# The last three experts of a mixture in plain fp32, from weights that are no longer split

## The chip, the cores and the metric

The kernel runs on one core of a Trainium2 chip. The metric is the device time of one execution in microseconds. Before the change it is 2594.24 us (median of 3 runs, 2590.64 to 2599.49). The five engines are named as in the profile: PE (TensorE), ACT (ScalarE), DVE (VectorE), POOL (GpSimd) and SP (SyncE), which here issues nearly all DMAs.

## What is computed

Four transformer blocks in a row, for one sequence of 256 tokens and a width of 1024, all in fp32. The change reaches the last part of the last block alone, a mixture of eight experts in which every token is sent to two:

```
def swiglu(h, w_gate, w_up, w_down):
    return (jax.nn.silu(h @ w_gate) * (h @ w_up)) @ w_down

def moe_swiglu(h, router, w_gate, w_up, w_down):          # h: 1 x 256 x 1024
    t = h.reshape(-1, d)
    logits = (t @ router).astype(jnp.float32)
    top_v, top_i = lax.top_k(logits, TOP_K)                # TOP_K = 2, N_EXPERTS = 8
    top_w = jax.nn.softmax(top_v, axis=-1)
    gates = jnp.sum(jax.nn.one_hot(top_i, N_EXPERTS, dtype=jnp.float32) * top_w[..., None], axis=1)
    out = jnp.zeros(t.shape, jnp.float32)
    for e in range(N_EXPERTS):
        y_e = swiglu(t, w_gate[e], w_up[e], w_down[e]).astype(jnp.float32)
        out = out + gates[:, e:e + 1] * y_e
    return out.astype(h.dtype).reshape(bsz, seq, d)
```

An expert has three matrices of 1024 x 3584 (gate, up) and 3584 x 1024 (down) in fp32, 44 MB together; all eight are 352 MB.

## The kernel before

**Places.** The experts are put in the order of how many tokens they have. The tokens of an expert are gathered by a product with a one-hot matrix (`moe_gather`, line 2171) into so many places: 128 for each of the first five experts, 64 for each of the last three (`PLACES`, line 1980). Below, the first are the wide experts, the last the narrow ones. A second pass for tokens that found no place is in the program, but does not run with this input.

**Weights.** An expert's matrices come in 42 loads of 1 MiB each, SBUF tiles of 128 partitions by 2048 fp32 values (line 217, issued by SP in program order). For gate and up a load holds two blocks of 128 rows by 1024 columns, in an expert's last step four blocks by 512. After landing in a `raw` buffer, ACT rounds the tile to fp32r (`wh`, line 222), and DVE takes what is left over (`wl = raw - wh`, line 223). After that `raw` is free, and SP may issue the next load into it. There are five `raw` buffers, three `wh` and three `wl` (`phase` with two more opened by `wider`, lines 2383, 2388 and 2401).

**Products.** An operand is a sum of two fp32r parts, too. For a wide expert three products are made, high by high, high by rest, rest by high (`mm3`, lines 229 to 231), 128 columns of the stationary operand by 512 moving ones. For a narrow expert the 64 columns of both parts of the tokens stand side by side in one stationary operand of 128 columns, and two products with `wh` and with `wl` (line 2263) leave two halves of the PSUM partitions, 0 to 63 and 64 to 127, which are folded by a copy and an add (`whole`, lines 2286 and 2287, tile `eb`). A load thus costs 12 products with a wide expert and 8 with a narrow one.

**Order.** An expert's 3584 hidden columns are done in four steps (three of 1024, one of 512). Step i goes: gate product of step i + 1, transposes of step i's hidden values (`turn`, line 2311), up product of step i + 1, down product of step i. At the end of an expert `combine` brings its rows back to the tokens with four pairs of products (lines 2347 and 2348) and adds them, weighted, to the sum (line 2349). So the first narrow expert's first 8 loads stand ahead of the last 2 loads of the last wide expert. The kernel ends with the four stores of line 2167.

**Other places that are referred to.** Lines 727, 728, 751 and 752 belong to an earlier block and are not touched. They are plain fp32 products: line 727 is one product of 128 stationary by 256 moving columns, line 728 one by 128; lines 751 and 752 are, for each of two heads, a product of 64 stationary columns by 256 (751) and by 128 (752) moving ones, the first head's result in PSUM partitions 0 to 63, the second's in 64 to 127.

Of the kernel before, what the change touches and what calls it, by code (L numbers as in the profile page):

```python
# [22 lines left out]
ND = 8  # L23
# [31 lines left out]
class Core:  # L55
# [65 lines left out]
    @contextmanager  # L121
    def phase(s, raw, split, work):

        with ExitStack() as c:
            pool = lambda nm, n: c.enter_context(s.tc.tile_pool(name=f"{nm}{s.uid()}", bufs=n, reuse_waits="tile"))
            s.ring = {nm: [pool(nm, n)] * n for nm, n in (("raw", raw), ("wh", split), ("wl", split))}
            s.t2p = pool("t2", work)
            yield

    @contextmanager  # L130
    def wider(s, **more):

        with ExitStack() as c:
            for nm, n in more.items():
                p = c.enter_context(s.tc.tile_pool(name=f"{nm}{s.uid()}", bufs=n, reuse_waits="tile"))
                s.ring[nm].extend([p] * n)
            s.turn = 0
            yield

    turn = 0  # L140
# [1835 lines left out]
class MoE:  # L1976
# [125 lines left out]
    def moe(s, N):  # L2102
# [6 lines left out]
        s.moe_pass(N, N.slot, s.PLACES, s.TOGETHER, first, ahead)  # L2109
# [3 lines left out]
        with s.tc.If(n > 0):  # L2113
            rest = s.small([128, 2, s.E], "slotb")
            nc.vector.tensor_sub(rest, N.slot, bc(s.caps, 2))
            s.moe_pass(N, rest, s.REST, s.TOGETHER_REST, s.moe_gather(N, rest, s.TOGETHER_REST[0], s.REST))
            s.moe_store()
# [52 lines left out]
    def moe_gather(s, N, slot, js, places):  # L2170
# [20 lines left out]
        for d in range(0, ND, 2):  # L2191
            p = s.psum("b")
            for m in range(2):
                for h, src in enumerate((N.H, N.L)):
                    for t in range(2):
                        nc.tensor.matmul(p[:, m * W:m * W + W], src[d // 2][:, t, m * 128:m * 128 + 128], P[:, t, :W],
                                         start=(h == 0 and t == 0 and m == 0), stop=(h == 1 and t == 1),
                                         skip_group_check=True)
            for m in range(2):
                x = s.t2([128, 512], "xe", F32R)  # L2200
                x = x[:, :2 * W].rearrange("p (a j c) -> p j a c" if wide else "p (j a c) -> p j a c", a=2, j=len(js))
                v, g = p[:, m * W:m * W + W].rearrange("p (j c) -> p j c", j=len(js)), s.col("ln_ffn_2", 8 + d + m)
                nc.scalar.activation(x[:, :, 0], v, AF.Copy, scale=g)
                nc.vector.scalar_tensor_tensor(x[:, :, 1], v, g, f(x[:, :, 0]), op0=OP.mult, op1=OP.subtract)
                X.append(x)
        return {j: [X, i, places[j], P] for i, j in enumerate(js)}

    def moe_places(s, N, G):
# [4 lines left out]
        n = next(iter(G.values()))[2]  # L2213
        for X, i, n, P in G.values():
            for t in range(2):
                nc.tensor.matmul(p[:n, i:i + 1], f(P[:, t, i * n:i * n + n]), N.rc[:, t:t + 1], start=(i == 0 and t == 0),
                                 stop=(t == 1), skip_group_check=True)
        nc.vector.tensor_copy(rc[:n], p[:n, :len(G)])
        for g in G.values():
            X, i, n, P = g  # L2220
            PT = s.t2([128, 2, 128], "onehotT", F32R)
            x = P[:, :, i * n:i * n + n]
            if n == 64:
                y = s.t2([128, 512], "eyH", F32R)[:, :256].rearrange("p (t c) -> p t c", t=2)
                for u in range(2):
                    nc.vector.tensor_copy(y[:, :, u * 64:u * 64 + 64], f(x))
                x = y
            p = s.psum("b", dt=F32R)
            for t in range(2):
                nc.tensor.transpose(p[:, t * 128:t * 128 + 128], x[:, t], s.identR)  # L2230
            nc.scalar.copy(PT, p[:, :256].rearrange("p (t c) -> p t c", t=2))
            g += [PT, rc[:n, i:i + 1]]

    AHEAD = 3
    WIDE = 1024

# [4 lines left out]
    def moe_pass(s, N, slot, places, together, G, ahead=()):  # L2241
# [3 lines left out]
        steps = [(j, f0, min(s.WIDE, s.FE - f0)) for j in range(s.E) for f0 in range(0, s.FE, s.WIDE)]  # L2245
        per = len(steps) // s.E
        py = {}
        ahead = list(ahead)
        most = places is s.PLACES
        src = {nm: I[f"o_moe_w_{nm}_2"][0] for nm in ("gate", "up", "down")}  # L2250

        def weights(nm, j, *a):
            e = N.expert[j]
            w = src[nm]
            return s.weights(w[e] if isinstance(e, int) else w[bass.ds(e, 1)].rearrange("o r c -> (o r) c"), *a)

        def product(o, j, x, w, start, stop):


            if x.shape[2] == 64:  # L2260
                x = x.rearrange("p a c -> p (a c)")
                for h in range(2):
                    nc.tensor.matmul(o, x, w[h], start=start and h == 0, stop=stop and h == 1, skip_group_check=True)  # L2263
            else:
                s.mm3(o, (x[:, 0], x[:, 1]), w, start, stop)

        def half(i, nm):

            j, f0, fn = steps[i]
            X, u = G[j][:2]  # L2270
            p = [s.psum("a") for _ in range(fn // 512)]
            nk = 2048 // fn
            for k0 in range(0, ND, nk):
                w = ahead.pop(0) if ahead else weights(nm, j, 128 * k0, nk, f0, fn)
                for k in range(nk):
                    for c, o in enumerate(p):
                        product(o, j, X[k0 + k][:, u], [x[:, k, c * 512:c * 512 + 512] for x in w],
                                k0 + k == 0, k0 + k == ND - 1)
            return p

        def whole(p, n):

            if n == 128:
                return p
# [3 lines left out]
            return a  # L2288

        def gate(i, pg):  # L2290
            n, rc = G[steps[i][0]][2], G[steps[i][0]][5]
            out = []
            for p in pg:
                out.append(s.t2([n, 512], "eh"))
                nc.scalar.activation(out[-1], whole(p, n), AF.Silu, scale=rc)
            return out

        def hidden(i, h, pu):
            n, rc = G[steps[i][0]][2], G[steps[i][0]][5]
            for x, p in zip(h, pu):  # L2300
                nc.vector.scalar_tensor_tensor(x, whole(p, n), rc, x, op0=OP.mult, op1=OP.mult)
            return h

        def turn(i, h):

            n = G[steps[i][0]][2]
            out = []
            for x in h:
                p = s.psum("b")
                for k in range(4):  # L2310
                    nc.tensor.transpose(p[:, k * n:k * n + n], x[:, k // 2 * 256 + k % 2:k // 2 * 256 + 256:2],
                                        s.ident[:n, :n])
                v = p[:, :4 * n].rearrange("p (k c) -> p k c", k=4)
                if n == 128:
                    H, L = s.t2([128, 4, n], "ehH", F32R), s.t2([128, 4, n], "ehL", F32R)
                else:
                    x = s.t2([128, 4, 2, n], "ehHL", F32R)
                    H, L = x[:, :, 0], x[:, :, 1]
                s.split(v, H, L)
                out.append((H, L) if n == 128 else x)  # L2320
            return out

        def down(i, hs):
            j, f0, fn = steps[i]
            if f0 == 0:
                py[j] = [s.psum("b"), s.psum("b")]
            for k0 in range(0, fn // 128, 2):
                w = weights("down", j, f0 + 128 * k0, 2, 0, D, "p k")
                h = hs[k0 // 4]
                for k in range(2):  # L2330
                    kk = k0 % 4 + k
                    for c in range(2):
                        wc = [x[:, k, c * 512:c * 512 + 512] for x in w]
                        start, stop = f0 == 0 and k0 + k == 0, f0 + fn == s.FE and k0 + k == fn // 128 - 1
                        if isinstance(h, tuple):
                            s.mm3(py[j][c], (h[0][:, kk, :], h[1][:, kk, :]), wc, start, stop)
                        else:
                            product(py[j][c], j, h[:, kk], wc, start, stop)

        def combine(j):  # L2340
            PT = G[j][4]
            for c in range(2):
                yH, yL = s.t2([128, 512], "eyH", F32R), s.t2([128, 512], "eyL", F32R)
                s.split(py[j][c], yH, yL)
                for t in range(2):
                    p = s.psum("b")
                    nc.tensor.matmul(p, PT[:, t, :], yH, start=True, stop=False)
                    nc.tensor.matmul(p, PT[:, t, :], yL, start=False, stop=True)
# [4 lines left out]
        pg = half(0, "gate")  # L2353
# [4 lines left out]
        h = hidden(0, h, half(0, "up"))  # L2358
        for i in range(n):
            j, f0, fn = steps[i]  # L2360
            if f0 == s.WIDE and j + 1 < s.E and j + 1 not in G:
                g = s.moe_gather(N, slot, next(x for x in together if j + 1 in x), places)
                s.moe_places(N, g)
                G |= g
            pg = half(i + 1, "gate") if i + 1 < n else None
            hs = turn(i, h)
            if pg is not None:
                h = gate(i + 1, pg)
                h = hidden(i + 1, h, half(i + 1, "up"))
            down(i, hs)  # L2370
# [58 lines left out]
```

## Time and profile before

| | |
|---|---|
| median of 3 runs | 2594.24 us |
| profiled execution | 2596.73 us, its span 2595.0 us |
| granted TensorE clock over the span | 0.968 of full speed |
| PE, DVE, ACT busy | 2423.1, 2004.4, 1550.8 us |
| read from memory | 555.88 MB, 215 GB/s over the span |

The mixture takes the last 40% of the span: the page's line of GB/s jumps from 131 to 343 in slice 26 of 40. A busy share is an average over all stages, and for DMA it says that packets were underway, not how many loads stood ready behind them. An engine's idle time only costs something where somebody waits for it; what ends a wait is in the views of waits.

### The profile page before, as it was taken

Reading aid. Unit: us, or ns where it says so; the run is one execution under the profiler, and the core shown is the slowest. Engines: PE = TensorE matmul, PEld = TensorE weight load, DVE = VectorE, ACT = ScalarE, POOL = GpSimd, SP = SyncE. Lnnn points to the kernel's source line nnn. Section 1 sums busy time; section 2 is a strip of 40 time slices with the busy share of each in tenths; the row PEclk is TensorE's granted clock in tenths of the full one; section 3 lists DMA queues with packets and bytes.
Section 4 is the critical chain, followed back from the end, with each engine's and each line's share of the span. In section 5 each row is a group of like instructions: output and inputs, shape, how many; then the busy total and the mean of one; then the engine's idle time right before and its main releaser. Section 6 shows DMA issues by size and latency. Waiting matters only on the chain.

```text
span 2595.0 us, 39887 instructions
## 1 busy us (share of the span) xinstructions
PE 2423.1 (93%) x15462; PEld 2122.8 (82%) x15462; DVE 2004.4 (77%) x3186; ACT 1550.8 (60%) x2313; POOL 88.0 (3%) x180
## 2 busy tenths in 40 slices
PE   7988799999998999899999999999999999988887
PEld 6867689999888999789999888888888877655654
DVE  6876477658886765766658876888888888999998
ACT  4553355445555544564455645776777777878776
POOL 2011010000001000000000000000000000000000
PEclk9998699999999999989999998999999999999999
DMA  5312345555434555425554213999999998999997
GB/s 166 111 58 34 62 166 167 178 178 162 131 109 137 165 178 183 146 82 184 183 172 130 87 45 131 343 359 349 368 329 365 346 360 325 371 379 363 372 369 281
DMA packets 266195, 559.59 MB, mean 216 GB/s; under 512 B 12751, under 2 KB 172510, under 8 KB 251662
## 3 DMA queue, kind: packets, MB, share of 16 engines
q1 hardware_dynamic: 264544, 555.71, 61.2%
q0 software_dynamic: 1328, 1.22, 0.9%
q8 instruction: 123, 2.02, 0.3%
q14 instruction: 74, 0.61, 0.1%
q10 hardware_dynamic: 126, 0.03, 0.0%
HBM read 555.88 MB, written 1.05 MB: 215 GB/s over the span
## 4 chain that ended last, share of the span: by engine, by line
PE 69%; DVE 15%; issue 6%; ACT 4%; POOL 2%; DMA 2%; DVEq 0%; ACTq 0%; POOLq 0%; SPq 0%
PE pa L230 16%; PE pa L231 16%; PE pa L229 16%; DVE wl L223 9%; ACT wh L222 2%; PE pb L230 2%; PE pb L231 2%; PE pb L229 2%; PE pb L1167 2%; PE pb L1792 2%; PE pa L2263 1%; PE pb L1481 1%; PE pb L2263 1%; PE pb L1133 1%; DMA ssmvb<-in_ssm_a_log_dram 1%
## 5 line engine op out<-in xcount | busy, mean ns | idle before, releaser
L223 DVE TENSOR_TENSOR wl<-raw,wh 128x512 fp32r<-128x512 f32 (+1 forms) x1108 | 1258.7, 1166 | 212.3 <-ACT wh L222 207.1
L222 ACT CAST wh<-raw 128x512 fp32r<-128x512 f32 (+1 forms) x1108 | 1063.6, 1004 | 559.3 <-issue 266.3
L229 PE MATMUL pa<-xH,wh 128*128 128x256 f32 (+1 forms) x1936 | 553.2, 286 | 16.0 <-ACT xH L313 8.1
L230 PE MATMUL pa<-xL,wh 128*128 128x256 f32 (+1 forms) x1936 | 553.3, 286 | 0.5 <-DVE xL L314 0.5
L231 PE MATMUL pa<-xH,wl 128*128 128x256 f32 (+1 forms) x1936 | 552.8, 286 | 1.0 <-DVE wl L223 1.0
L229 PEld LDWEIGHTS pa<-xH,wh 128*128 128x128 f32 (+1 forms) x1936 | 372.3, 193 | 18.1 <-ACT xH L313 8.8
L230 PEld LDWEIGHTS pa<-xL,wh 128*128 128x128 f32 (+1 forms) x1936 | 372.3, 192 | 3.5 <-DVE xL L314 2.0
L231 PEld LDWEIGHTS pa<-xH,wl 128*128 128x128 f32 (+1 forms) x1936 | 372.2, 192 | 2.9 <-DVE wl L223 1.9
L230 PE MATMUL pa<-wl,xe 128*128 128x512 f32 x560 | 221.1, 395 | 7.7 <-DVE wl L223 7.7
L231 PE MATMUL pa<-wh,xe 128*128 128x512 f32 x560 | 219.7, 392 | 0.0
L229 PE MATMUL pa<-wh,xe 128*128 128x512 f32 x560 | 207.7, 393 | 0.0
L2263 PE MATMUL pa<-wl,xe 128*128 128x512 f32 x336 | 131.2, 424 | 36.8 <-DVE wl L223 34.0
L229 PE MATMUL pa<-hidH,wh 128*128 128x256 f32 x528 | 149.4, 283 | 0.0
L230 PE MATMUL pa<-hidL,wh 128*128 128x256 f32 x528 | 149.4, 283 | 0.0
L231 PE MATMUL pa<-hidH,wl 128*128 128x256 f32 x528 | 149.4, 283 | 0.0
L230 PEld LDWEIGHTS pa<-wl,xe 128*128 128x128 f32 x560 | 105.7, 189 | 34.0 <-DVE wl L223 12.8
L2263 PE MATMUL pa<-wh,xe 128*128 128x512 f32 x336 | 123.7, 402 | 3.5 <-ACT wh L222 3.5
L229 PEld LDWEIGHTS pa<-wh,xe 128*128 128x128 f32 x560 | 105.6, 189 | 21.3
L231 PEld LDWEIGHTS pa<-wh,xe 128*128 128x128 f32 x560 | 105.6, 189 | 21.0
L2263 PEld LDWEIGHTS pa<-wl,xe 128*128 128x128 f32 x336 | 59.6, 192 | 76.3 <-DVE wl L223 67.0
L230 PE MATMUL pb<-wl,ehH 128*128 128x512 f32 x280 | 111.2, 397 | 0.9 <-DVE wl L223 0.9
L231 PE MATMUL pb<-wh,ehL 128*128 128x512 f32 x280 | 109.4, 391 | 0.0
(813 smaller groups left out, 4078.8 us busy)
## 6 DMA issues: line engine op xcount, KB each, us to landing
raw<-in_o_moe_w_gate_dram SPq DMA_DIRECT2D x112, 1024.0 KB
raw<-in_o_moe_w_up_dram SPq DMA_DIRECT2D x112, 1024.0 KB
raw<-in_o_moe_w_down_dram SPq DMA_DIRECT2D x112, 1024.0 KB
raw<-in_ffn_w_dram SPq DMA_DIRECT2D x60, 1024.0 KB
raw<-in_od_w_in_dram SPq DMA_DIRECT2D x20, 1024.0 KB
raw<-in_o_w_in_dram SPq DMA_DIRECT2D x16, 1024.0 KB
raw<-in_e_ffn_w_gate_dram SPq DMA_DIRECT2D x11, 1024.0 KB
raw<-in_e_ffn_w_up_dram SPq DMA_DIRECT2D x11, 1024.0 KB
```

The lines of the kernel that those rows point to most:

```text
L222: nc.scalar.copy(H[:, c:e], raw[:, c:e])
L223: nc.vector.tensor_sub(L[:, c:e], raw[:, c:e], f(H[:, c:e]))
L229: mm(out, a[0], b[0], start=start, stop=False, skip_group_check=True)
L230: mm(out, a[0], b[1], start=False, stop=False, skip_group_check=True)
L231: mm(out, a[1], b[0], start=False, stop=stop, skip_group_check=True)
L1133: nc.tensor.matmul(p[:, k * 128:k * 128 + 128], NT[:, k, :], X[:, k, :], start=True, stop=True)
L1167: mm = lambda o, a, b, st=True, sp=True: nc.tensor.matmul(o, a, b, start=st, stop=sp, skip_group_check=True)
L1481: mm = lambda o, a, b, st, sp: nc.tensor.matmul(o, a, b, start=st, stop=sp, skip_group_check=True)
L1792: mm = lambda o, a, b, st=True, sp=True: nc.tensor.matmul(o, a, b, start=st, stop=sp, skip_group_check=True)
L2263: nc.tensor.matmul(o, x, w[h], start=start and h == 0, stop=stop and h == 1, skip_group_check=True)
```

## The change

For a narrow expert a load is no longer split. `whole_weights` loads it, and PE reads it as it lies there, in plain fp32. The gathered tokens are kept as one fp32 tile (`xf`) of 64 columns an expert. A row block of a load now gives two products of 64 stationary columns: one half of the moving columns goes to PSUM partitions 0 to 63, the other half to 64 to 127. SiLU and product then run on [128, 512] tiles at once; four transposes bring them to `ehT`. Since nothing is split, the `wh` and `wl` buffers can take loads as well: `KINDS` gives the order in which loads go to the eleven buffers, each ring with its own turn (`buffer`). `moe_gather` and `moe_places` double the one-hot matrix, so that both halves find their rows; `combine` uses plain fp32 products with 64 rows. The wide experts' code does as before; the second pass is called in another way and still does not run.

```
+    def buffer(s, nm):
+        i = s.turns[nm]
+        s.turns[nm] += 1
+        return s.ring[nm][i % len(s.ring[nm])].tile([128, 2048], F32 if nm == "raw" else F32R, tag=nm,
+                                                    name=f"{nm}{s.n}")
...
-        raw, H, L = (s.ring[nm][s.turn % len(s.ring[nm])].tile([128, 2048], dt, tag=nm, name=f"{nm}{s.n}")
-                     for nm, dt in (("raw", F32), ("wh", F32R), ("wl", F32R)))
-        s.turn += 1
+        raw, H, L = (s.buffer(nm) for nm in ("raw", "wh", "wl"))
...
+    def whole_weights(s, src, k0, nk, c0, cn, rows="k p", kind="raw"):
+        s.n += 1
+        raw = s.buffer(kind)
+        v = f(raw)[:, :nk * cn].rearrange("p (k c) -> p k c", k=nk)
+        s.nc.sync.dma_start(v, src[k0:k0 + 128 * nk, c0:c0 + cn].rearrange(f"({rows}) c -> p k c", p=128))
+        return v
...
+                else:
+                    nc.scalar.activation(y[:, m], v, AF.Copy, scale=g)
+                    X.append(y[:, m].rearrange("p (j c) -> p j c", c=64))
...
+    KINDS = ("raw", "wh", "raw", "wl", "raw", "wh", "raw", "wl", "raw", "wh", "wl")
...
+            return s.weights(w, *a) if places[j] == 128 else s.whole_weights(w, *a, kind=next(kinds))
...
-            if x.shape[2] == 64:
-                x = x.rearrange("p a c -> p (a c)")
-                for h in range(2):
-                    nc.tensor.matmul(o, x, w[h], start=start and h == 0, stop=stop and h == 1, skip_group_check=True)
...
+                        for c in range(2):
+                            mm(p[0][64 * c:64 * c + 64, :hw], X[k0 + k][:, u], w[:, k, c * hw:c * hw + hw],
+                               start=start, stop=stop, skip_group_check=True)
...
-            a = s.t2([64, 512], "eb")
-            nc.scalar.copy(a, p[64:])
-            nc.vector.tensor_add(a, p[:64], a)
...
+                    y = s.t2([128, n, 128], "ehT")
+                    nc.scalar.copy(y, v)
...
+                        for c in range(2):
+                            mm(py[j][0][64 * c:64 * c + 64], hs[0][:, q, 64 * a:64 * a + 64],
+                               w[:, k, c * 512:c * 512 + 512], start=start, stop=stop, skip_group_check=True)
...
+            if not wide:
+                y = s.t2([128, 512], "ey")
+                nc.scalar.copy(y, py[j][0])
...
+                        mm(p, f(PT[64 * c:64 * c + 64, t, :]), y[64 * c:64 * c + 64], start=True, stop=True)
```

PE's queue at the first load of the first narrow expert, before: one load, eight products, `xe` the stationary operand with both parts.

```order
L2263 MATMUL pa_22594<-wh_22597,xe_22099 128x512
L2263 MATMUL pa_22594<-wl_22598,xe_22099 128x512
L2263 MATMUL pa_22595<-wh_22597,xe_22099 128x512
L2263 MATMUL pa_22595<-wl_22598,xe_22099 128x512
L2263 MATMUL pa_22594<-wh_22597,xe_22102 128x512
L2263 MATMUL pa_22594<-wl_22598,xe_22102 128x512
L2263 MATMUL pa_22595<-wh_22597,xe_22102 128x512
L2263 MATMUL pa_22595<-wl_22598,xe_22102 128x512
```

The same place now: four products a load (x4), all to one PSUM tile, the first from a `raw` buffer, the second from a `wh` buffer, and so on; line 2335 is the transposes of the last wide step.

```order
L2307 MATMUL pa_22582<-raw_22583,xf_22099 64x512 x4
L2307 MATMUL pa_22582<-wh_22589,xf_22111 64x512 x4
L2307 MATMUL pa_22582<-raw_22595,xf_22123 64x512 x4
L2335 MATMUL pb_22607<-ident,eh_22470 128x128 x4
L2307 MATMUL pa_22582<-wl_22601,xf_22135 64x512 x4
L2307 MATMUL pa_22618<-raw_22619,xf_22099 64x512 x4
```

What stood in eight products by 512 columns, alternately with `wh` and `wl`, are now four with 64 columns from one buffer.

SP's queue at the same place, before: every load goes into a `raw` buffer, and the two last loads of the last wide expert (down) come after the narrow expert's first eight.

```order
L217 DMA raw_22596<-in_o_moe_w_gate_dram 128x2x1024
L217 DMA raw_22610<-in_o_moe_w_gate_dram 128x2x1024
L217 DMA raw_22624<-in_o_moe_w_gate_dram 128x2x1024
L217 DMA raw_22638<-in_o_moe_w_gate_dram 128x2x1024
L217 DMA raw_22673<-in_o_moe_w_up_dram 128x2x1024
```

And now (line 236 is `whole_weights`, line 222 `weights`):

```order
L236 DMA raw_22583<-in_o_moe_w_gate_dram 128x2x1024
L236 DMA wh_22589<-in_o_moe_w_gate_dram 128x2x1024
L236 DMA raw_22595<-in_o_moe_w_gate_dram 128x2x1024
L236 DMA wl_22601<-in_o_moe_w_gate_dram 128x2x1024
L236 DMA raw_22619<-in_o_moe_w_up_dram 128x2x1024
```

The loads and their order are the same; the buffers alternate, and the second load goes into a `wh` buffer.

## Rows read from the trace of the kernel before

**Rows 1.** The page: its span, and the span in 40 slices.

```profile
span 2595.0 us, 39887 instructions
...
DVE  6876477658886765766658876888888888999998
...
DMA  5312345555434555425554213999999998999997
```

**Rows 2.** Stages: stretch in us, then busy us (and instructions) by engine, clock, DMA.

```profile
core 0: us, PE busy (x) PEld busy (x) DVE busy (x) ACT busy (x) POOL busy (x), PEclk, DMA share, GB/s
2000.00:2100.00 100.00, 98.61 (x446) 81.24 (x445) 88.92 (x53) 71.67 (x49) 0.00 (x0) 1.00 0.96 353
2212.00:2570.00 358.00, 303.39 (x1161) 211.32 (x1160) 341.14 (x232) 281.47 (x219) 0.00 (x0) 0.97 0.99 373
2225.50:2583.90 358.40, 301.86 (x1146) 207.79 (x1145) 340.85 (x230) 279.66 (x218) 0.00 (x0) 0.97 0.96 362
```

**Rows 3.** Groups by line, 2225.5 to 2583.9: busy us, mean ns, idle before.

```profile
L223 DVE TENSOR_TENSOR wl<-raw,wh 128x2048 fp32r<-128x2048 f32 x127 | 285.5, 2283 | 12.1 <-ACT wh L222 11.5
L222 ACT CAST wh<-raw 128x2048 fp32r<-128x2048 f32 x126 | 237.4, 1906 | 20.3 <-PE pb L2263 8.8 <-DMA raw<-in_o_moe_w_up_dram 4.2 <-DMA raw<-in_o_moe_w_gate_dram 3.3
...
L2287 DVE TENSOR_TENSOR eb<-pa,eb 64x512 f32<-64x512 f32 x42 | 27.7, 677 | 4.1 <-ACT eb L2286 4.1
L2286 ACT COPY eb<-pa 64x512 f32<-64x512 f32 x42 | 23.4, 579 | 41.9 <-PE pa L2263 41.8
```

**Rows 4.** What SP's DMA queue waited for, 2212 to 2570: us, times, longest.

```profile
SPq L217 <- DVE wl L223: 258.3, 113, 5.1
SPq L217 <- DVE ehHL L291: 29.1, 14, 2.3
```

**Rows 5.** Short stretches of the narrow stage, and one early stretch.

```profile
2295.00:2307.00 12.00, 9.07 (x36) 6.06 (x35) 10.80 (x7) 9.62 (x8) 0.00 (x0) 1.00 1.02 421
2350.00:2370.00 20.00, 15.23 (x57) 9.73 (x56) 18.89 (x14) 17.01 (x14) 0.00 (x0) 1.00 1.02 414
2414.00:2426.00 12.00, 9.09 (x36) 6.05 (x35) 10.80 (x7) 9.62 (x8) 0.00 (x0) 1.00 1.03 424
2470.00:2484.00 14.00, 11.02 (x43) 7.29 (x42) 12.81 (x10) 11.91 (x11) 0.00 (x0) 1.00 1.02 414
2526.00:2546.00 20.00, 16.31 (x63) 10.92 (x62) 18.65 (x11) 15.79 (x14) 0.00 (x0) 1.00 1.02 416
2546.00:2556.00 10.00, 8.78 (x34) 6.54 (x33) 10.00 (x10) 8.48 (x7) 0.00 (x0) 0.83 0.98 356
2333.00:2340.00 7.00, 5.38 (x23) 3.54 (x22) 6.43 (x6) 6.97 (x6) 0.00 (x0) 1.00 0.76 243
2500.00:2514.00 14.00, 11.75 (x41) 8.24 (x40) 14.00 (x12) 11.12 (x11) 0.00 (x0) 0.88 0.92 315
274.60:322.30 47.70, 45.06 (x247) 38.20 (x248) 24.46 (x76) 17.48 (x49) 2.08 (x2) 0.61 0.20 70
```

**Rows 6.** PE in order of time, plain fp32: start us, length us, then the group.

```profile
634.50 0.60 PE L727 MATMUL pb<-bc,bc 128*128 128x256 f32 x2
634.93 0.38 PE L728 MATMUL pb<-bc,bc 128*128 128x128 f32 x2
...
647.38 0.66 PE L751 MATMUL pb<-mt,xd 128*64 128x256 f32 x4
647.86 0.40 PE L752 MATMUL pb<-mt,xd 128*64 128x128 f32 x4
```

**Rows 7.** PE in order of time: last wide loads' first product, first narrow one.

```profile
2214.89 0.39 PE L229 MATMUL pb<-wh,ehH 128*128 128x512 f32 x1
...
2225.76 0.39 PE L2263 MATMUL pa<-wh,xe 128*128 128x512 f32 x1
```

**Rows 8.** SP's DMA issues in order of time, from the first narrow load.

```profile
2210.31 9.49 SPq L217 DMA_DIRECT2D raw<-in_o_moe_w_gate_dram  x4
...
2543.34 2.58 SPq L217 DMA_DIRECT2D raw<-in_o_moe_w_gate_dram  x2
2550.26 2.57 SPq L217 DMA_DIRECT2D raw<-in_o_moe_w_up_dram  x2
```

**Rows 9.** The end, in order of time.

```profile
2568.82 0.33 SPq L217 DMA_DIRECT2D raw<-in_o_moe_w_down_dram  x1
...
2583.53 0.40 PE L2263 MATMUL pb<-wl,ehHL 128*128 128x512 f32 x1
2585.40 2.73 DVE L2349 SCALAR_TENSOR_TENSOR hT<-pb,gates,hT 128x512 f32<-128x512 f32 x4
2586.18 3.33 SPq L2167 DMA_DIRECT2D out_dram<-hT  x4
```

More of the change, by code (lines that the diff above doesn't have):

```diff
@@ L1 @@
+import itertools
 import math
@@ L2108, in moe @@
         s.moe_order(N)
-        s.moe_pass(N, N.slot, s.PLACES, s.TOGETHER, first, ahead)
+        s.moe_pass(N, first, ahead)
         s.moe_store()
@@ L2212, in moe_places @@
         p = s.psum("b")
-        n = next(iter(G.values()))[2]
+        Y = []
         for X, i, n, P in G.values():
[L2215 to L2222, printed above, removed]
+            y = P[:, :, i * n:i * n + n]
@@ L2223, in moe_places @@
             if n == 64:
-                y = s.t2([128, 512], "eyH", F32R)[:, :256].rearrange("p (t c) -> p t c", t=2)
+                x, y = y, s.t2([128, 2, 128], "onehotD", F32R)
                 for u in range(2):
                     nc.vector.tensor_copy(y[:, :, u * 64:u * 64 + 64], f(x))
-                x = y
+            Y.append(y)
+            for t in range(2):
+                nc.tensor.matmul(p[:, i:i + 1], f(y[:, t]), N.rc[:, t:t + 1], start=(i == 0 and t == 0),
+                                 stop=(t == 1), skip_group_check=True)
@@ L2234, with moe_pass, moe_lane @@
     AHEAD = 3
     WIDE = 1024
+    KINDS = ("raw", "wh", "raw", "wl", "raw", "wh", "raw", "wl", "raw", "wh", "wl")
     def moe_weights(s, i):
         return s.weights(s.i["o_moe_w_gate_2"][0, 0], 256 * i, 2, 0, s.WIDE)
-    def moe_pass(s, N, slot, places, together, G, ahead=()):
+    def moe_pass(s, N, first, ahead):
+        for _ in s.moe_lane(N, N.slot, s.PLACES, s.TOGETHER, first, ahead, True):
+            pass
+    def moe_lane(s, N, slot, places, together, G, ahead=(), most=False):
         nc = s.nc
@@ L2244, in moe_pass @@
         I = s.i
-        steps = [(j, f0, min(s.WIDE, s.FE - f0)) for j in range(s.E) for f0 in range(0, s.FE, s.WIDE)]
-        per = len(steps) // s.E
+        G = dict(G)
+        mm = nc.tensor.matmul
+        js = [j for x in together for j in x]
+        steps = [(j, f0, min(s.WIDE, s.FE - f0)) for j in js for f0 in range(0, s.FE, s.WIDE)]
+        per = len(steps) // len(js)
         py = {}
         ahead = list(ahead)
-        most = places is s.PLACES
         src = {nm: I[f"o_moe_w_{nm}_2"][0] for nm in ("gate", "up", "down")}
+        kinds = itertools.cycle(s.KINDS)
@@ L2309, in turn @@
                 p = s.psum("b")
[L2310 to L2315, printed above, removed]
-                else:
[L2317 to L2320, printed above, removed]
+                n = x.shape[1] // 128
+                for k in range(n):
+                    nc.tensor.transpose(p[:, k * 128:k * 128 + 128], x[:, k // 2 * 256 + k % 2:k // 2 * 256 + 256:2],
+                                        s.ident)
+                v = p[:, :n * 128].rearrange("p (k c) -> p k c", k=n)
+                if wide:
+                    H, L = s.t2([128, n, 128], "ehH", F32R), s.t2([128, n, 128], "ehL", F32R)
+                    s.split(v, H, L)
+                    out.append((H, L))
+                else:
+                    y = s.t2([128, n, 128], "ehT")
+                    nc.scalar.copy(y, v)
+                    out.append(y)
             return out
@@ L2340, in combine @@
         def combine(j):
             PT = G[j][4]
+            wide = places[j] == 128
+            if not wide:
+                y = s.t2([128, 512], "ey")
+                nc.scalar.copy(y, py[j][0])
             for c in range(2):
-                yH, yL = s.t2([128, 512], "eyH", F32R), s.t2([128, 512], "eyL", F32R)
-                s.split(py[j][c], yH, yL)
+                if wide:
+                    yH, yL = s.t2([128, 512], "eyH", F32R), s.t2([128, 512], "eyL", F32R)
+                    s.split(py[j][c], yH, yL)
@@ L2357, in moe_pass @@
         h = gate(0, pg)
-        h = hidden(0, h, half(0, "up"))
+        h = inner(0, h, (yield from half(0, "up")))
         for i in range(n):
             j, f0, fn = steps[i]
-            if f0 == s.WIDE and j + 1 < s.E and j + 1 not in G:
-                g = s.moe_gather(N, slot, next(x for x in together if j + 1 in x), places)
+            if f0 == s.WIDE and i + per < n and steps[i + per][0] not in G:
+                g = s.moe_gather(N, slot, next(x for x in together if steps[i + per][0] in x), places)
                 s.moe_places(N, g)
                 G |= g
-            pg = half(i + 1, "gate") if i + 1 < n else None
+            pg = (yield from half(i + 1, "gate")) if i + 1 < n else None
             hs = turn(i, h)
@@ L2368, in moe_pass @@
                 h = gate(i + 1, pg)
-                h = hidden(i + 1, h, half(i + 1, "up"))
-            down(i, hs)
+                h = inner(i + 1, h, (yield from half(i + 1, "up")))
+            yield from down(i, hs)
             if f0 + fn == s.FE:
```

98 lines of the change are left out of this document (53 added, 45 removed).

## The prediction

> **What bounds the kernel now.** I read the page first, then the stages, then the groups of the one stage that the change reaches, then the waits of the DMA queue. The page [rows 1] gives a span of 2595.0 us; in the last fifteen of its forty slices DMA stands at 8 or 9 (7 in the last) and VectorE at 8 or 9. That suggests two limits at once, so the stages decide. With 128 places (2000 to 2100) PE is busy 98.6 of 100 us at 353 GB/s. With 64 places (2225.5 to 2583.9) PE is busy 301.9 of 358.4 us, VectorE 340.9, and the DMA share of the longer part is 0.99 at 373 GB/s [rows 2]. So the wide experts are bound by PE. The narrow ones are bound by VectorE or by the loads, and the share does not tell which.
>
> The groups tell VectorE's part: 127 splits of 2283 ns are 285.5 of its 340.9 us, and the folding adds (`eb`) 27.7 more [rows 3]. The waits of the DMA queue settle it: out of the 358 us from 2212, SP stood 258.3 us in 113 waits for line 223, VectorE's split, which gives the load buffer back, and 29.1 us for another VectorE line [rows 4]. A load is issued only when VectorE is done with a buffer. The 0.99 is a mean busy share with a load or two underway; it is no ceiling. Short stretches show that [rows 5]: while loads are queued, the same engines move 414 to 424 GB/s (five stretches of 12 to 20 us), and where buffers are late, 243 and 315. A 1 MiB load takes 1.0486 MB / 414 GB/s = 2.53 us, against the 2.84 us it takes now: issues run from 2210.3 for load 0 to 2568.8 for load 125 of the narrow experts, with two wide loads among them, so (2568.8 - 2210.3) / 127 = 2.82 [rows 8, 9], and PE's 358.4 us / 126 = 2.84 [rows 2].
>
> **What the change removes.** 126 casts of 1906 ns on ACT and 126 subtractions of 2283 ns on VectorE, the folding copies and adds, and with them VectorE's hold on the load buffers. VectorE and ACT keep little in this stage (about 21 SiLU passes, 21 products, 42 transposes' copies), under 60 us each in 330.
>
> **What it adds on PE.** A load now needs four plain fp32 products of 64 columns by 512, in two pairs, instead of eight split products. A plain fp32 product leaves two records: line 727 is one product of 256 moving columns, stands as x2, and the next line starts 634.93 - 634.50 = 0.43 us later [rows 6]. For 512 columns that is 0.86 us, an estimate by doubling. Two such products with 64 stationary columns each, to the two halves of the PSUM partitions, stand in line 751 (x4, that is two products): the next pair starts 647.86 - 647.38 = 0.48 us later, where one behind the other they would take 0.86 [rows 6]. So the halves run together. A load then costs PE 2 x 0.86 = 1.72 us; one behind the other it would be 3.44. I take 1.72, since line 751 is the same form (128 rows, 64 columns, fp32, neighbouring halves); the bounds are 1.72 and 3.44. With the few transposes and the twelve products of the combining steps (0.86 each) PE has 126 x 1.72 + about 20 = 237 us of work, less than any sum of the loads below: PE waits for loads, and what PE does costs nothing as long as a pair stays under about 2.5 us per load.
>
> **What the eleven buffers do.** Each is free as soon as PE has used it, about 2 us after it landed, so eight to ten loads are queued at any time. I therefore take the rate of the queued stretches. For the 12 loads of the last steps (four rows of 2 KB per partition) the nearest row is the stretch from 2546, in which two such loads follow two others that were issued from 2543.3 on: 356 GB/s, 2.95 us, measured with a short queue [rows 5, 8]; I take 2.75 for these and 2.55 (412 GB/s) for the other 115 of the 127: 293.3 + 33.0 = 326.3 us. Bounds: 424 GB/s gives 314 us; today's 373 gives 357.
>
> **What is late at the switch.** The second narrow load goes into a `wh` buffer. Only three exist and the last wide loads are split into them, so it waits until PE has used the third wide load from the end. SP takes its loads in order, so all later ones wait behind it, `raw` ones too. PE runs the last four wide loads from 2214.89 to 2225.76, 2.72 us each; the second of them ends at 2214.89 + 5.44 = 2220.3 [rows 7]. Today loads 1, 2 and 3 are issued in that time (four issues from 2210.31, 9.49 us long) [rows 8]. So the change starts with a loss: load 0 at 2210.3 as today, the other 127 from 2220.3. Two of these are wide ones; they still pass ACT and VectorE, and the narrow loads behind them find their `wh` and `wl` buffers late. For that I add 2 us (between 0 and the 5.4 us that PE needs for the two). The earlier gather and the doubled one-hot matrices fall into the wide stage, where VectorE and ACT have room (89 and 72 of 100 us) beside a full PE: nothing.
>
> **The end.** Now the last load is issued at 2568.82, and what has landed is still split and worked off until PE's last product, which starts at 2583.53 and ends at 2583.9 [rows 9]. After the change one load is left when the last has landed: 1.72 us. From there to the end it is 2595.0 - 2583.9 = 11.1 us now. Two casts and two subtractions go; a copy (about 0.58, the mean of line 2286 [rows 3]) and four fp32 products in place of eight split ones come, two row halves that may or may not run together (1.7 or 3.4 us), ahead of the same four adds and stores. The end comes to between 10.1 and 11.9; I take 11.8.
>
> **Sum.** 2220.3 + 326.3 + 2 + 1.7 + 11.8 = 2562 us, 33 below the span. The profiled run took 2596.73 us, 1.7 above its span and 2.5 above the median of 2594.24; against that median the forecast is 2594.2 - 33 = 2561 us.
>
> **Rivals.**
> 1. *The memory gives no more than now.* For it: a share of 0.99 at 373 GB/s over 358 us. Against it: the five stretches above 413 and SP's 287 us of waits for VectorE. Then 127 x 2.81 = 357 us and 2220.3 + 357 + 15.5 = 2593 us of span, 2 less than before: about 2592, no change. The Trainium skill speaks for this rival ("DMA: Bandwidth & Descriptors", Specifications): it puts the memory's share of one core at about 358 GB/s, by which, as an estimate, 127 loads would take 372 us and the kernel some 13 us longer than now. This trace disagrees: 373 GB/s over 358 us and 424 over 12 us. A middle case, 385 to 395 GB/s, gives 2573 to 2580.
> 2. *PE becomes the bound, and the kernel slower.* Place: the narrow stage. Either the two halves run one behind the other, or PE, which now waits most of a microsecond at each load, is granted 1.2 GHz instead of 2.4. Both price a load at 3.44 us: 2225.8 + 126 x 3.44 + 5.4 + 12 = 2677 us of span, about 2676 against the median. It decides against the change from about 2.8 us per load on. For the clock: from 274.6 to 322.3 PE was busy 45 of 47.7 us and yet had 0.61 of the full clock [rows 5]. Against it: in the narrow stage PE has gaps at every load today, 57 of 358 us, at a granted 0.97 [rows 2]; and a PE at 1.2 GHz would have no gaps left, and only a mix that leaves less than a load per 2.57 us costs time: with two thirds of the stage at 1.2 GHz it is still (1/3) / 1.72 + (2/3) / 3.44 = 0.388 loads per us, one in 2.58 us. The Trainium skill ("TensorE: Matmul & The Clock Gate", HAM oscillation) tells of kernels whose matmuls come in bursts between loads and lose the full clock each time; by it this rival would be likelier than the rows make it.
> 3. *The switch between wide and narrow costs more*, 8 to 15 us instead of 2, because wide loads, narrow loads and SP's order block each other, or PE's row of transposes, SiLU and product at each step holds buffers longer than eleven cover. Against it: eleven buffers are 28 us of loads. Then 2569 to 2575.
>
> **How the numbers follow.** Forecast (queued rate, halves together): 0.68, its own range 2551 to 2569. Rival 3 and the middle rate: 0.18. Rival 1: 0.08. Rival 2: 0.06. About 0.3% (8 us) is what a measurement of this kernel can tell from no change. Faster: the forecast, rival 3 and the middle rate, less a little for the slow end of the last: 0.86. Same: rival 1, 0.08. Slower: 0.06. The range for 8 in 10 goes from 2550 (424 GB/s throughout and no loss at the switch) to 2581 (a middle rate with a costly switch).
>
> **What would show it.** Right: in the narrow stage about 400 to 415 GB/s over 300 us, SP waiting for PE instead of VectorE, PE's products as pairs that start together with some 0.86 us from pair to pair, PE's idle time ahead of them put down to the DMA of `raw`, `wh` and `wl`, a bump of low DMA rate near 2213 to 2222, and the last load landing near 2548. Wrong: 1.72 us from pair to pair, or a granted clock near 0.5 through the stage (rival 2); 370 to 385 GB/s with loads always queued (rival 1); SP or PE idle for several microseconds between 2220 and 2260 (rival 3).

## The result and the profile after

The changed kernel took 2565.77 us (median of four runs, 2560.47 to 2566.34); the kernel before took 2596.39 us on the same chip (2590.64 to 2599.49). The ratio is 0.988, with a 95% interval of 0.9857 to 0.9903: 25 to 37 us less, 30.6 by the medians, where 33 were forecast. The profiled execution, the shortest of the four, took 2560.47 us with a span of 2558.8 us, 36.2 below the span of before [rows 1].

First the page of the changed kernel: span, VectorE and DMA in forty slices, beside [rows 1].

```profile
span 2558.8 us, 39340 instructions
...
DVE  6876486658886765666657886888898988610000
...
DMA  5310355555435455525554322899999998899998
GB/s 163 118 59 34 38 178 165 183 167 164 132 116 166 129 189 170 177 67 182 185 166 144 100 67 83 306 336 353 369 348 345 347 363 326 341 410 409 411 412 330
```

VectorE is nearly gone from the last five slices. In the first four of them the loads run at 409 to 412 GB/s; the last also holds the end, behind the last load. The stages say it more exactly; columns are start and end, length, busy us (and count) of PE, its weight loads, VectorE, ACT and POOL, the granted clock, DMA's share and GB/s. Under the heading, the first row is the time from the first narrow load's issue to the second's, the second the narrow loads from there on, the third goes against the last row but one of [rows 2], the fourth is a steady stretch, and the last two are the second, parted at 2262.

```profile
core 0: us, PE busy (x) PEld busy (x) DVE busy (x) ACT busy (x) POOL busy (x), PEclk, DMA share, GB/s
2206.50:2216.70 10.20, 10.20 (x46) 8.45 (x45) 9.10 (x7) 7.67 (x7) 0.00 (x0) 1.00 0.53 218
2216.70:2546.00 329.30, 267.92 (x1216) 91.13 (x1216) 24.98 (x30) 20.63 (x31) 0.00 (x0) 0.99 1.01 405
2212.00:2550.00 338.00, 275.93 (x1251) 96.12 (x1249) 30.02 (x35) 24.91 (x35) 0.00 (x0) 0.99 0.99 395
2300.00:2400.00 100.00, 79.61 (x368) 24.42 (x366) 4.80 (x7) 4.67 (x8) 0.00 (x0) 1.00 1.03 410
2216.70:2262.00 45.30, 38.23 (x146) 17.75 (x146) 11.88 (x11) 6.24 (x6) 0.00 (x0) 0.92 0.99 390
2262.00:2545.80 283.80, 229.56 (x1070) 73.26 (x1066) 13.10 (x19) 14.39 (x25) 0.00 (x0) 1.00 1.02 408
```

VectorE fell to 25 us of 329. The DMA share, 0.99 before at 373 GB/s, is 1.01 now at 405: the share said nothing of room. What SP waited for in the stage, as line and releaser with the us in total, how often and the longest, answers to [rows 4]:

```profile
SPq L236 <- PE pa L2307: 51.8, 27, 4.5
SPq L236 <- PE pb L2364: 50.2, 16, 8.0
...
SPq L236 <- DVE wl L228: 11.7, 3, 5.8
SPq L236 <- PE pb L244: 10.2, 4, 4.6
```

258 us of waits for VectorE became 102 us of waits for the narrow products (43 waits), and 65 us more that are put down to loads still landing. They cost nothing in the steady stretch, where other loads are queued and the rate is 410. The two last lines are the switch. It stands in SP's issues beside [rows 8] (start, us, line, what):

```profile
2206.49 0.38 SPq L236 DMA_DIRECT2D raw<-in_o_moe_w_gate_dram  x1
2216.70 0.38 SPq L236 DMA_DIRECT2D wh<-in_o_moe_w_gate_dram  x1
2217.29 0.37 SPq L236 DMA_DIRECT2D raw<-in_o_moe_w_gate_dram  x1
...
2227.45 0.39 SPq L236 DMA_DIRECT2D raw<-in_o_moe_w_gate_dram  x1
2235.70 0.38 SPq L236 DMA_DIRECT2D wh<-in_o_moe_w_gate_dram  x1
...
2241.37 0.37 SPq L236 DMA_DIRECT2D raw<-in_o_moe_w_gate_dram  x1
2250.28 0.37 SPq L236 DMA_DIRECT2D wh<-in_o_moe_w_up_dram  x1
```

and in GB/s by slices of 3 us from 2205 to 2325, where the hole is about 6 us wide:

```profile
GB/s 431 410 115 0 186 425 419 403 406 410 427 419 401 412 414 325 416 419 408 426 423 421 401 412 410 406 412 411 411 422 426 415 402 385 387 388 423 423 415 408
```

PE's timeline (start, us, products, in brackets the idle time before and what ended it) goes with [rows 6]; its first row, the first product of the last four wide loads, goes with [rows 7]:

```profile
2211.07 0.39 PE L242 MATMUL pb<-wh,ehH 128*128 128x512 f32 x1
...
2222.04 1.94 PE L2307 MATMUL pa<-raw,xf 128*64 128x512 f32 x8
2223.81 1.89 PE L2307 MATMUL pa<-wh,xf 128*64 128x512 f32 x8
2225.52 1.89 PE L2307 MATMUL pa<-raw,xf 128*64 128x512 f32 x8
...
2233.72 1.94 PE L2307 MATMUL pa<-wh,xf 128*64 128x512 f32 x8 [0.62 <-DMA wh<-in_o_moe_w_up_dram]
2236.28 1.94 PE L2307 MATMUL pa<-raw,xf 128*64 128x512 f32 x8 [0.62 <-DMA raw<-in_o_moe_w_up_dram]
```

On line 2307, x8 are a load's four products. Where loads lie ready, one load follows the other after 2223.81 - 2222.04 = 1.77 and 1.71 us; where they don't, after 2.56 us, with PE waiting for the load. The end, as the chain that ended last (start, us, what), beside [rows 9]:

```profile
2525.66 20.17 DMA raw<-in_o_moe_w_down_dram
2545.83 0.04 issue
2545.88 1.96 PE pb L2364 x8
2547.84 0.02 issue
2547.86 0.59 ACT ey L2373
2548.45 0.04 issue
2548.50 2.04 PE pb L2384 x8
2550.54 0.89 DVE hT L2385 x2
```

The last load stood 20.17 us between issue and landing, some eight loads of 2.56 us deep in the queue; behind it is one load's product, a copy, the combining products and the adds.

### The profile page after: what moved, and what is told of

The parts are those of the page before. It is cut to its first block, busy times and chain, and to the rows that moved or that the text cites. A ratio compares the mean times of both kernels' runs of the same rounds, so it can differ in the third digit from the quotient of the medians.

```text
span 2558.8 us, 39340 instructions
## 1 busy us (share of the span) xinstructions
PE 2382.6 (93%) x15516; PEld 2000.3 (78%) x15516; DVE 1679.8 (66%) x2974; ACT 1287.6 (50%) x2124; POOL 88.6 (3%) x180
## 4 chain that ended last, share of the span: by engine, by line
PE 71%; DMA 11%; DVE 8%; issue 4%; ACT 3%; POOL 2%; SPq 0%; ACTq 0%; POOLq 0%; DVEq 0%
PE pa L243 16%; PE pa L244 16%; PE pa L242 16%; DVE wl L228 3%; PE pb L243 3%; PE pb L244 2%; PE pb L242 2%; DMA raw<-in_o_moe_w_down_dram 2%; DMA wl<-in_o_moe_w_down_dram 2%; PE pb L1180 2%; PE pb L1805 2%; DMA wh<-in_o_moe_w_down_dram 2%; ACT wh L227 1%; PE pa L2307 1%; PE pb L1494 1%
## 5 line engine op out<-in xcount | busy, mean ns | idle before, releaser
L228 DVE TENSOR_TENSOR wl<-raw,wh 128x512 fp32r<-128x512 f32 (+1 forms) x982 | 974.4, 1021 | 204.3 <-ACT wh L227 199.9
L227 ACT CAST wh<-raw 128x512 fp32r<-128x512 f32 (+1 forms) x982 | 826.1, 888 | 549.7 <-issue 266.3
L242 PEld LDWEIGHTS pa<-xH,wh 128*128 128x128 f32 (+1 forms) x1936 | 372.4, 193 | 18.2 <-ACT xH L326 8.8
L243 PE MATMUL pa<-wl,xe 128*128 128x512 f32 x560 | 220.9, 395 | 7.7 <-DVE wl L228 7.7
L244 PE MATMUL pa<-wh,xe 128*128 128x512 f32 x560 | 219.4, 392 | 0.0
L2323 DVE SCALAR_TENSOR_TENSOR eh<-pa,slotrc,eh 128x512 f32<-128x512 f32 (+1 forms) x47 | 33.4, 733 | 267.1 <-PE pa L2307 259.4
L242 PE MATMUL pa<-wh,xe 128*128 128x512 f32 x560 | 207.7, 393 | 0.0
L243 PEld LDWEIGHTS pa<-wl,xe 128*128 128x128 f32 x560 | 105.6, 189 | 33.9 <-DVE wl L228 12.8
L242 PE MATMUL pb<-wh,ehH 128*128 128x512 f32 x280 | 102.0, 393 | 2.5 <-ACT wh L227 2.5
L2317 ACT ACTIVATE eh<-pa,slotrc 128x512 f32<-128x512 f32 (+1 forms) x47 | 30.7, 674 | 145.3 <-PE pa L2307 125.8
```

The costliest lines, as they stand in the source:

```text
L242: mm(out, a[0], b[0], start=start, stop=False, skip_group_check=True)
L243: mm(out, a[0], b[1], start=False, stop=False, skip_group_check=True)
L244: mm(out, a[1], b[0], start=False, stop=stop, skip_group_check=True)
L2317: nc.scalar.activation(out[-1], p, AF.Silu, scale=rc)
L2323: nc.vector.scalar_tensor_tensor(x, p, rc, x, op0=OP.mult, op1=OP.mult)
```

## The experiments

The theory: VectorE's split held the load buffers, so too few loads were queued; unsplit, loads are always queued and the memory gives some 410 GB/s. Against it stood that the memory or PE bounds the stage, that the six further buffers do the work, and that the switch still costs what could be saved. "Load 0 to the end" below is the time from the issue of the first of the last 128 loads to the end of the span: 384.7 us in the profile of before, 352.3 and 352.5 in two profiled executions of the changed kernel. It leaves out what happens ahead of the switch, by which profiles of one and the same kernel differ: in the two profiles of `raw` buffers first (below) that issue came at 2202.75 and 2206.91 us, while the time behind it differs by 0.2 us. Times are against the kernel before on the same chip, intervals 95%.

**Five buffers, unsplit.**

```
-    KINDS = ("raw", "wh", "raw", "wl", "raw", "wh", "raw", "wl", "raw", "wh", "wl")
+    KINDS = ("raw",)
```

> The narrow experts' loads go into the five raw buffers alone (as many as before the change), unsplit, the rest as in the changed kernel. Theory (before, VectorE's long hold on the buffers kept loads back, not their number): PE gives a buffer back about 2 us after landing, so three to four loads stay queued; 395 to 410 GB/s in the steady part of the narrow stage, at most 10 us slower than the changed kernel (2560 to 2576 us), since the second narrow load no longer waits for a wh buffer (6 us gained) but five buffers cannot cover PE's two wide loads (some 8 us lost). Rival (eleven buffers make the rate): 370 to 380 GB/s and 2585 to 2595 us.

2564.01 us, ratio 0.9871 (0.9854 to 0.9887); load 0 to the end 356.1 us. Stage and SP's waits:

```profile
2300.00:2400.00 100.00, 79.83 (x370) 25.03 (x368) 5.55 (x8) 5.25 (x9) 0.00 (x0) 1.00 1.02 410
```

```profile
SPq L236 <- PE pa L2307: 162.7, 82, 10.6
SPq L236 <- PE pb L2364: 70.7, 37, 2.9
```

The rate of the changed kernel with as many load buffers as before. So the split was the cause, not the number of buffers, and 373 GB/s was not the memory's bound. How much of it was VectorE's own work and how much its hold on the buffers, this run does not tell apart. SP waits more than twice as long (233 us against 102), and in the stage that costs nothing. Load 0 to the end is 3.8 us longer than in the changed kernel, so five buffers aren't quite as good as eleven; the loss lies at the switch, where the rate falls to 126 GB/s in one slice of 9 us.

**Three buffers.**

```
+    KINDS = ("wh",)
```

> The narrow experts' loads go into the three wh buffers alone. Theory (the rate depends on how many loads are queued): with one buffer in PE's hands about two are queued; 375 to 400 GB/s in the steady part, SP waiting for PE at every load, the switch later as well; 2572 to 2592 us. Rival (the rate is the memory's own and needs no queue): 405 GB/s or more and under 2570 us.

2637.33 us, ratio 1.0159 (1.0134 to 1.0185): slower than before. The five executions lie between 2621.21 and 2645.26 us, and the profile is of the shortest.

```profile
2300.00:2400.00 100.00, 73.68 (x330) 22.93 (x326) 4.80 (x7) 4.66 (x8) 0.00 (x0) 0.97 0.95 358
2400.00:2500.00 100.00, 69.16 (x318) 21.69 (x314) 2.62 (x4) 3.39 (x6) 0.00 (x0) 0.98 0.98 361
```

The direction was expected, the size was not: 358 to 361 GB/s at shares of 0.95 and 0.98. Neither PE nor VectorE is full, and only the number of buffers was changed, so the rate follows the number of loads queued; between three and five buffers lies the step. Why it fell so much further than expected stays open.

**Products one behind the other.** In all but the last row block of each sum, the second half's products go to the first half's partitions, so that the two no longer lie on different halves. The same is done in the down product.

```
...
+    one = c == 1 and not stop
+    o = p[0][:64, :hw] if one else p[0][64 * c:64 * c + 64, :hw]
...
```

> In all but the last row block of each sum, the second half's product goes to PSUM partitions 0 to 63 as well, so that two products of a pair cannot run side by side (the sums of the two halves are mixed by that; number and size of the products stay). Theory (side by side saves half of PE's time, and PE becomes the bound without it): 3.2 to 3.4 us of PE per load, 126 of them about 413 us, PE busy without gaps in the narrow stage, DMA at 310 to 330 GB/s; 2650 to 2675 us. Rival (PE has room whichever way they run): under 2575 us.

2671.28 us, ratio 1.0279 (1.0262 to 1.0296). Stage, and PE's timeline:

```profile
2300.00:2400.00 100.00, 100.00 (x283) 36.82 (x283) 1.98 (x3) 3.68 (x7) 0.00 (x0) 1.00 0.93 325
```

```profile
2301.95 3.60 PE L2309 MATMUL pa<-wl,xf 128*64 128x512 f32 x8
2305.38 3.60 PE L2309 MATMUL pa<-raw,xf 128*64 128x512 f32 x8
```

2305.38 - 2301.95 = 3.43 us a load at the full clock, PE without a gap. That is rival 2 as priced (3.44 us, 2676): the change stands on the two halves running together. Without that it would have been a loss.

**Half the products.** Every second row block is left out of the narrow products, in gate, up and down.

```
...
-                        for c in range(2):
+                        for c in range(2) if k % 2 == 0 else ():
...
```

> Every second row block of a narrow expert's loads is left out of the products (loads, buffers and everything else as in the changed kernel; half of the sum is missing in these experts). Theory (the narrow stage is now bound by the rate of the loads, PE only follows): PE's work per load falls from 1.72 to 0.86 us and the time stays within 3 us of the changed kernel's, 2561 to 2567 us; DMA at 408 to 412 GB/s in the steady part. Rival (PE's products still set part of the pace, by the holding of buffers or by a chain through the steps): 10 us or more below, under 2555 us.

2557.14 us, ratio 0.986 (0.9837 to 0.9882); load 0 to the end 352.9 us.

```profile
2300.00:2400.00 100.00, 68.93 (x195) 15.01 (x194) 4.80 (x7) 5.25 (x9) 0.00 (x0) 0.69 1.02 410
2400.00:2500.00 100.00, 66.10 (x196) 15.69 (x194) 5.55 (x8) 4.57 (x8) 0.00 (x0) 0.72 1.02 411
```

Same time, same rate: PE is not the bound. It freed less of PE than meant, though, for the granted clock fell to 0.69 and 0.72, a mix of 2.4 and 1.2 GHz, and PE's busy time only from 80 to 66 to 69 us in 100. So the clock part of rival 2 is real in this run, where products come as short bursts between loads; it cost no time here, where PE still had 31 to 34 us of 100 idle. The Trainium skill ("TensorE: Matmul & The Clock Gate", HAM oscillation) describes such a loss of clock; this run agrees as to the clock (0.69 and 0.72) and shows no loss of time, and the changed kernel itself kept 0.99.

**The switch: `raw` buffers first.** The first five narrow loads go to `raw` buffers and need no `wh` or `wl` buffer; measured twice, the second time beside the changed kernel on the same chip.

```
+    KINDS = ("raw", "raw", "raw", "raw", "raw", "wh", "wl", "wh", "wl", "wh", "wl")
```

> Same eleven buffers, but the first five narrow loads take the raw ones, then wh and wl in turn. Theory (the changed kernel loses some 6 to 10 us at the switch because its second narrow load waits for a wh buffer and SP takes loads in order): narrow loads 1 to 4 are issued from about 2209 on instead of 2216 to 2219, no dip of the DMA rate there, 4 to 7 us less than the changed kernel: 2558 to 2562 us if that one is at its median of 2565.8. Rival (the lost time is made up later, or the two wide loads in between set the pace): within 2 us of the changed kernel.

> The changed kernel once more, on the chip and beside the runs of e9 and e11, to compare them without the difference between chips: 0.986 to 0.990 of the time before, 2560 to 2568 us.

> e3 once more, beside the changed kernel. Theory (raw buffers first saves some of the wait at the switch): 2 to 7 us less than e10. Rival (the difference of e3 came from the spread between executions): within 1 us of e10.

First 2558.45 us, ratio 0.9859 (0.9842 to 0.9877). Then the changed kernel again took 2557.8 us, ratio 0.9849 (0.9824 to 0.9873), and this one 2557.51 us, 0.984 (0.9818 to 0.9862): the medians are 0.3 us apart, so the rival came, and the changed kernel itself came out some 2 us below the 2560 to 2568 that I had expected of it. Load 0 to the end is 350.2 and 350.0 us against 352.3 and 352.5: some 2 us less in both pairs of profiles, which the times can't tell from nothing. The first run's 7 us against the changed kernel's first median lie within the spread of the changed kernel's five executions here (2553.68 to 2565.71). The number of the first expectation came (2558 to 2562 us), its reason did not, as slices of 3 us from 2205 to 2325 of the first profile show:

```profile
GB/s 403 370 348 343 363 411 411 421 421 287 313 184 287 418 416 410 412 425 418 421 406 411 410 411 410 408 411 419 426 421 409 382 387 388 413 426 421 408 410 412
```

The hole of the changed kernel is gone, but a second one, down to 184 GB/s, has come some 25 us later, and most of what was saved goes there.

**The switch: wide loads first.** As above, and the last wide expert's two loads for the down product are issued ahead of all narrow loads; then the same with `raw` alone.

```
...
+            if i + 1 < n and places[j] == 128 and places[steps[i + 1][0]] == 64:
+                early.extend(weights("down", j, f0 + 128 * k0, 2, 0, D, "p k") for k0 in range(0, fn // 128, 2))
...
+                w = early.pop(0) if early else weights("down", j, f0 + 128 * k0, 2, 0, D, "p k")
```

> As e3_raw_first, and the last wide expert's two remaining loads are issued ahead of the first narrow ones, so that they are split by the time that PE comes to them. Theory (what is still lost at the switch is PE waiting for the split of these two, while it holds buffers, so that SP issues nothing for some 10 us): PE's gap of about 5 us ahead of the two wide loads goes, no dip of the DMA rate under 390 GB/s after 2220, 2 to 5 us less than e3: 2553 to 2557 us. Rival (the buffers cover that wait): within 1 us of e3, 2558 us.

> The five raw buffers alone, as in e1, and the last wide expert's two remaining loads issued ahead of the first narrow ones, as in e6. Theory (what the switch still costs in e3 and e6 is SP standing before a wh buffer that the wide loads' splits hold, with all later loads behind it): no wait for a split buffer is left, the DMA rate has no dip under 390 GB/s between 2225 and 2260, from the first narrow load's issue to the end 343 to 348 us in place of 352.3 (changed kernel), 350.2 (e3) and 356.1 (e1); 2552 to 2557 us. Rival (five buffers cannot cover a step's chain of transposes and SiLU without the wide loads' help): 352 us or more, as the changed kernel.

2557.13 us, ratio 0.9856 (0.9833 to 0.9878), and 2563.91 us, ratio 0.9874 (0.9855 to 0.9892); load 0 to the end 350.6 and 351.8 us. No gain over `raw` first (350.2 and 350.0), where the first expectation had 2 to 5 us. With `raw` alone I expected 343 to 348 us, since no load then waits for a `wh` buffer; that fell too. Slices of 3 us from 2205 to 2325 of that run:

```profile
GB/s 393 410 328 281 360 322 399 412 406 406 384 347 329 314 352 350 377 429 429 421 421 395 412 410 410 408 411 416 423 421 421 391 384 389 395 426 415 423 404 410
```

The hole is gone, and shallow dips to 281 and 314 stand in its place. From 2215 to 2260 SP waited mostly for the narrow products:

```profile
SPq L236 <- PE pa L2308: 27.4, 13, 3.1
```

They now stand between the wide loads' products in PE's queue. Whether that makes the dips is not shown.

**Wide and narrow woven.** The narrow experts' loads are spread among the wide ones (4 to 3), so that the memory's room under the PE-bound wide stage is used; then the same with `raw` alone.

```
...
+        s.weave(Task(s.moe_lane(N, N.slot, s.PLACES, s.TOGETHER[:-1], first, ahead, True), 4), Task(narrow(), 3))
```

> The changed kernel's code, but from the second expert on, the wide experts (12 products a load, PE's bound: 2.72 us against 2.56 for a load) and the narrow ones (1.72 us) run in turn, four wide loads and three narrow ones. Theory (the wide stage is bound by PE and the narrow one by loads, so each has room where the other has none): 294 loads x 2.56 = 752 us in place of 168 x 2.85 + 126 x 2.58 = 804; up to 50 us less, some of it lost to PSUM buffers, of which both now hold some: 2515 to 2550 us, DMA near 390 to 405 GB/s throughout. Rival (the shared PSUM and split buffers stop PE more often than the mixture gains): 2566 us or more.

> As e7_woven, with the narrow loads in the raw buffers alone, so that the wide experts keep the six split buffers. Theory (e1: five buffers are enough for the narrow loads; the split buffers are what the wide experts need): a few us below e7_woven, 2510 to 2545 us. Rival (five buffers for both kinds of loads are too few): above e7_woven.

2728.72 us, ratio 1.0529 (1.0502 to 1.0555), and 2649.95 us, 1.0212 (1.019 to 1.0233). Both failed; 2515 to 2550 and 2510 to 2545 us were expected. The first kernel's stage from 2000, and SP's longest sum of waits from 1800 to 2500:

```profile
2000.00:2100.00 100.00, 85.77 (x371) 57.36 (x370) 46.84 (x36) 39.85 (x37) 0.00 (x0) 0.90 0.73 286
```

```profile
SPq L236 <- DVE wl L228: 326.0, 30, 18.2
```

A narrow load that is due for a buffer still in a split stands at the head of SP's queue, up to 18.2 us, and everything behind it stands too; PE, which the weave was to keep full, is busy 85.8 us of 100 where it was 98.6 [rows 2]. The expectation's rival named PSUM as well; PE's longest waits from 1900 to 2500 are for splits (26.5 us for `wl`, 20.5 for `wh`), and none of note is for PSUM. With `raw` alone it is the wide loads that stand longest, 176.2 us in 64 waits for the split and 136.1 in 43 for narrow products: better, still slower than no weaving.

## Why the prediction came out right, step by step

**The bound.** Right, and shown: the five buffers of before, unsplit, give 410 GB/s. Reading SP's waits instead of DMA's share decided it. Rival 1 fell with that. The share of about 358 GB/s for one core that the Trainium skill gives ("DMA: Bandwidth & Descriptors", Specifications), half of a memory stack's rate, is no ceiling for this one core: it read at 405 GB/s over 329 us. Three buffers came to 358 and 361, by too few queued loads and not by a ceiling, since five gave 410.

**PE's 1.72 us per load.** Measured 1.71 and 1.77. Rival 2 was priced at 3.44 us and about 2676; its condition, one half behind the other, gave 3.43 us and 2671.28. PE's work as a whole was put too low, 237 us against 264 busy us (2222 to 2547.8): where PE waits ahead of a load, the load's products stand 1.94 us in the profile. That cost nothing, as was said of anything under about 2.5 us per load. The passes that VectorE and ACT keep were miscounted, also at no cost: 21, 21 and 42 were named, and 12 SiLU passes, 12 products and 12 transposes' copies ran, since they take tiles of 128 by 512 or 256.

**The sum.** It can be checked term by term from load 0 on, where the forecast was 2562 - 2210.3 = 351.7 us and the profile has 352.3. Load 0 to load 1: forecast 2220.3 - 2210.3 = 10.0, measured 2216.70 - 2206.49 = 10.2. The 127 loads with the 2 us of the switch: forecast 328.3, measured 2545.83 - 2216.70 = 329.1. Both parts of this term hold, so that no error hides another: from 2262 on the rate is 408 GB/s, which is the forecast's mean (127 x 1.0486 MB / 326.3 us = 408), and from 2216.7 to 2262 it is 390, which is 45.3 x (408 - 390) / 408 = 2.0 us lost. The last load on PE: 1.7 against 2.0. The tail: 11.8 against 2558.8 - 2547.84 = 11.0; the two row halves of the combining step do run together (four products in 1.99 us), which was left open between 1.7 and 3.4.

**The span.** It fell by 36.2 us where 33 were forecast: 32.4 of them lie behind load 0 (384.7 - 352.3). The other 3.8 lie ahead of it (2210.31 - 2206.49), where the forecast had nothing; two profiles of one kernel differ there by 4.2 us, so I take them for spread between executions.

**The eleven buffers** were given too much credit. The rate was right, the reason half so: about eight loads are queued at the end (the last stands 20.17 us), as forecast, but five buffers give the same 410 GB/s, and their whole loss is 3.8 us from load 0 to the end. Whether the split with more buffers would also have done was not tried; VectorE's 340.9 us of work in 126 loads [rows 2] is 2.71 us a load, so by this estimate it could win back at most (2.84 - 2.71) x 126 = 16 us of the 32. By the same estimate at least half of the gain comes from VectorE having less to do, and not from buffers being held for a shorter time.

**The switch.** The second narrow load's wait for a `wh` buffer came as worked out from the profile of before, down to its length: PE began its last four wide loads at 2211.07, the second ends at 2211.07 + 5.44 = 2216.5, and the load was issued at 2216.70. The sign set for rival 3 came too, SP idle for several microseconds between 2220 and 2260 (2227.84 to 2235.70, 2241.74 to 2250.28), without rival 3: the loads already queued kept the rate at 401 to 427 GB/s until 2250, with one slice of 325 behind it. Idle time of SP alone was no sign of a loss. How much of the switch can be had back I over-rated afterwards: the three kernels made for that gained 0.5 to 2.5 us from load 0 to the end in four profiles.

## What to carry to other kernels

A busy share of DMA near 1 is no sign of a full memory: look at what the load queue's waits are for, and at the rate in short stretches where loads are known to be queued. A change that frees load buffers earlier is worth the difference of these rates, up to the point where the number of queued loads no longer matters (here between three and five 1 MiB buffers). A load that must wait at the head of an in-order issue queue stops all behind it, so buffers that are freed at different speeds should not be taken in turn by one queue unless the slow ones are far ahead of need.

## What the runs showed of the hardware that I had not expected

- The rate of 1 MiB loads in this stage by buffers: three 358 to 361 GB/s, five 410 and 411, eleven 410 and 411, at DMA shares of 0.95 to 1.03.
- Two plain fp32 products of 64 stationary columns on different halves of the PSUM partitions take together what one takes (1.71 to 1.77 us for two pairs of 512 columns against 3.43), and so do two products of 64 rows in the combining step (four in 1.99 us).
- With half the products the granted clock fell from 1.00 to 0.69 and 0.72, and PE's busy time from 80 to 69 and 66 us of 100 in place of 40: two thirds of what leaving them out would have freed.
